# Prompt attention in the order in which it is written, on all engines and the sync queue

## The chip, the cores and the metric

The kernel runs on one core of one Trainium2 chip. The metric is the device time of one execution in microseconds (us). A core has five engines with an instruction stream each: PE (TensorE, matmuls and transposes), DVE (VectorE), ACT (ScalarE), POOL (GpSimd) and SP (SyncE, which here issues almost all DMAs). Each engine takes its own instructions in the order in which the built program holds them, and one that waits for another engine or for a DMA holds up all that stand behind it.

## The reference, cut to what matters

One layer of a hybrid trunk for a prompt of 2048 tokens and a small sample group. The part in question is the prompt's attention: 8 heads, and for each head three dilated patterns of 129 keys a query.

```
for (window, r) in ((128, 1), (512, 4), (2048, 16)):      # three patterns of each head
    scores = q . k[t], k[t-r], ..., k[t-window]  - slope * distance
    p = exp(scores - max);  out, lse = p @ v / sum(p), log-sum-exp
attn = sum over patterns of softmax(lse) * out
h = x + W_out [attn ; pool(n)]          # then y = h + ConvFFN(RMSNorm(h))
```

## The kernel before, in words

The kernel projects the prompt (queries, keys and values go to DRAM as `qT`, `kT`, `v_s`), does the attention, merges the three patterns and multiplies by `W_out`, and ends with the feed-forward part. This text is about the attention, from 447 to 813 us of the profiled execution.

Its work is a list of 192 **items**. Item `i` is two blocks of 128 queries of one head and one pattern, and each head has 24 items; head `h` begins at item 24 `h`. A block has one or two blocks of keys (narrow: 128 columns, wide: 256). An item goes through three steps, each an own function:

- `scores` (L289, L290): four matmuls into a PSUM tile `Sp` (four buffers); on DVE the bias and the minimum (`T`, `st`, L292); on ACT the exponential (`Pt`, L294).
- `turn` (L302): PE transposes `Pt` into a PSUM tile; the copy `PTs` out of it is on DVE for three items of four (L305) and on ACT for the fourth (L307).
- `values` (L324): matmuls with the value tile `V` into `Op`; ACT copies `Op` to `O` (L328), POOL adds `st` (L330), and after the last of a half, `store_o` sends `O` to DRAM on SP.

`advance(i)` writes down the scores of item `i`, the turn of item `i-2` and the values of item `i-3`, in this order. The first 8 calls of `advance` stand ahead of the changed loop. The loop calls `advance(i)` from 8 on, and writes other work ahead of some of the calls:

- at item 4 of head `h`, `load_head(h+1)`: six DMAs of 512 KB that bring the next head's `QK` tile (two buffers), and a bias table on POOL;
- at items of `NEXT_V`, `next_v`: the value tiles for the next pair of heads, 26 DMAs for each pair;
- `param_load` and `param_turn`, which bring parameters of the feed-forward part and transpose them on PE (L217);
- at items 150, 155, ..., 185 a piece of `W_out` for the next stage:

```
raw = p2.tile([P, CH], F32, tag="row", name="rawo", bufs=2)
nc.sync.dma_start(raw, wov[:, k, 0:CH])
split(wo0[k][:, 0, 0:CH], wo0[k][:, 1, 0:CH], raw)
```

`split` is a copy on ACT (L112, which waits for the DMA) and a subtraction on DVE (L113, which waits for the copy). In the kernel before, the written order is only a wish: the compiler's scheduler goes through the instructions with its own idea of how long each takes, and fixes the order on each engine. It places an instruction later than written where it takes its inputs to come late, and pulls others forward.

Of the kernel before, what the change touches and what calls it, by code (L numbers as in the profile page):

```python
# [9 lines left out]
F32 = mybir.dt.float32  # L10
# [7 lines left out]
P = 128  # L18
S = 2048
DM = 1024  # L20
KT = DM // P
H = 8
# [9 lines left out]
CH = 512  # L32
# [10 lines left out]
def f32(ap):  # L43
    return ap.bitcast(F32)
# [3 lines left out]
def kernel(ctx, tc, ins, cst, outs):  # L48
    nc = tc.nc
# [61 lines left out]
    def split(hi, lo, src, eng=None):  # L111
        nc.scalar.copy(hi, src)  # L112
        (eng or nc.vector).tensor_tensor(out=lo, in0=src, in1=f32(hi), op=ALU.subtract)  # L113
# [41 lines left out]
    def qk_tile():  # L155
        return pq.tile([P, 3, S], F32R, tag="QK", name="QK", bufs=2)

    def load_qk(h, qk, cols):
        rows = slice(h * DH, (h + 1) * DH)
        Q, KH, KL = (qk[:, i, cols] for i in range(3))  # L160
        nc.sync.dma_start(f32(Q[0:DH]), qT_hi[rows, cols])
        nc.sync.dma_start(f32(Q[DH:P]), qT_lo[rows, cols])
        for half in range(2):
            hr = slice(half * DH, (half + 1) * DH)
            nc.sync.dma_start(f32(KH[hr]), kT_hi[rows, cols])
            nc.sync.dma_start(f32(KL[hr]), kT_lo[rows, cols])

    def bias_table(h):
        tab = pq.tile([P, 3, 2 * P], F32, tag="tab", name="tab", bufs=2)
        nc.gpsimd.tensor_scalar(out=tab, in0=base, scalar1=2.0 ** -(h + 1), scalar2=None, op0=ALU.mult)  # L170
        return tab

    def value_tile(pool, tag):

        t = pool.tile([P, 8 if tag == "V" else 16, P + 2], F32, tag=tag, name="V", bufs=6 if tag == "V" else 1)
        nc.gpsimd.memset(t[:, :, 0:1], 1.0)
        nc.gpsimd.memset(t[:, :, P + 1:P + 2], 1.0)
        return t

    def load_v(hp, p, t, lo, hi):  # L180

        vs = v_s[:, hp * P:(hp + 1) * P]
        d = t[:, :, 1:P + 1]
        if p == 0:
            nc.sync.dma_start(d, vs.rearrange("(n i) f -> i n f", i=P)[:, lo:hi])
        else:
            r = DILS[p]
            n = min(r, hi - lo)
            for j in range(lo, hi, n):
                J, c = divmod(j, r)  # L190
                src = vs[J * P * r:(J + 1) * P * r].rearrange("(m c i) f -> i m c f", c=r, i=RUN)[:, :, c:c + n]
                for i in range(RUN):
                    nc.sync.dma_start(d[i::RUN, j - lo:j - lo + n, :], src[i])
# [4 lines left out]
    def param_load(j):  # L198
        n = 2 * NF if j < 4 else 2 * SB
        row = rows_of[j] = p2.tile([2 * NF, 4 * P], F32, tag="row", name="row", bufs=2)  # L200
        if j < 4:
            src = conv_b if j == 3 else conv_w[0, j:j + 1]
            nc.sync.dma_start(row[:, 0:P], src.rearrange("l (c p) -> (l c) p", p=P))
        else:
            nc.sync.dma_start(row[:n], stv[:, (j - 4) * 4 * P:(j - 3) * 4 * P])

    def param_turn(j):
        row = rows_of.pop(j)
        tp = psum.tile([P, 4, P], F32, tag="tp", name="tpc", bufs=4)
        if j < 4:  # L210
            n = 2 * NF
            nc.tensor.transpose(tp[:, 0, :n], row[:, 0:P], ident[:n, :n])
            nc.vector.tensor_copy(cw[:, j, :], tp[:, 0, :n])
        else:
            n = 2 * SB
            for c in range(4):
                nc.tensor.transpose(tp[:, c, :n], row[:n, c * P:(c + 1) * P], ident[:n, :n])  # L217
            nc.vector.tensor_copy(stT[:, 4 * j - 16:4 * j - 12, 0:n], tp[:, :, :n])
# [24 lines left out]
    def load_head(h):  # L243
        qk, tab = qk_tile(), bias_table(h)
        load_qk(h, qk, slice(0, S))
        heads[h] = (*(qk[:, i, :] for i in range(3)), tab)
# [3 lines left out]
    def next_v(hp, p, half):  # L250
        t = value_tile(p2, "V")
        load_v(hp, p, t, 8 * half, 8 * half + 8)
        for b in range(8):
            pair_v[hp, p, 8 * half + b] = t[:, b, :]
# [20 lines left out]
    def scores(it):  # L275
        h, p, pr = it
        tab = heads[h][3]
        if pr % 4 == 0:
            state["st", p] = pq.tile([P, 8], F32, tag="st", name="st", bufs=8)
        st = state["st", p]  # L280
        Sp = psum.tile([P, 2, 2 * P], F32, tag="mm", name="Sp", bufs=4)
        Pt = pq.tile([P, 2, 2 * P], F32, tag="P", name="Pt", bufs=3)
        blocks = []
        for s in range(2):
            idx = 2 * pr + s
            i8 = idx % 8
            q, kh, kl, kb = views(h, p, idx)
            w = P * len(kb)
            nc.tensor.matmul(Sp[:, s, :w], q, kh, start=True, stop=False)  # L289
            nc.tensor.matmul(Sp[:, s, :w], q, kl, start=False, stop=True)  # L290
            T = pq.tile([P, 2 * P], F32, tag="T", name="T", bufs=3)
            nc.vector.tensor_tensor_reduce(out=T[:, :w], in0=Sp[:, s, :w], in1=tab[:, p, 2 * P - w:], op0=ALU.add,  # L292
                                           op1=ALU.min, scale=1.0, scalar=3e38, accum_out=st[:, i8:i8 + 1])
            nc.scalar.activation(Pt[:, s, :w], T[:, :w], AF.Exp, bias=st[:, i8:i8 + 1], scale=-1.0)  # L294
            blocks += [(s, idx % 4, n, b, len(kb)) for n, b in enumerate(kb)]
        return st, Pt, blocks
# [40 lines left out]
    def turns(seq):  # L337
        at = {}
        for p in seq:
            n = at[p] = at.get(p, -1) + 1  # L340
            yield from ((p, 2 * n), (p, 2 * n + 1))

    ORDER = [(0, 0, 0, 0) + (2, 1) * 4] + [(0, 2, 1) * 4] * (H - 2) + [(0, 2, 2, 1, 2, 0, 2, 1, 0, 1, 1, 0)]
    items = [(h, p, pr) for h in range(H) for p, pr in turns(ORDER[h])]
    NI = 24
    AHEAD = 8
# [3 lines left out]
    def spread_next(i):  # L350
        if i < len(items):
            h, p, pr = items[i]
            if p and pr % 2 == 0:
                spread_q(h, p, pr // 2)

    def advance(i):
        if i >= AHEAD:
            spread_next(i + SPREAD)
        if i < len(items):
            attn[i] = scores(items[i])  # L360
        if 0 <= i - 2 < len(items):
            PTs[i - 2] = turn(items[i - 2], attn[i - 2])
        if 0 <= i - 3 < len(items):
            values(items[i - 3], attn.pop(i - 3), PTs.pop(i - 3))
# [4 lines left out]
    with tc.tile_pool(name="p1", bufs=1) as p1:  # L369
        raw, W_hi, W_lo = {}, {}, {}  # L370
# [326 lines left out]
    def act_tile(i):  # L697
        return (p4 if i % 2 else ph).tile([P, 2, 4, CH], F32R, tag="act", name="act", bufs=1)

    def load_pool(c):  # L700
        mB = act_tile(c)
        nc.sync.dma_start(f32(mB.rearrange("p a g t -> p (a g) t")),
                          pl_s.rearrange("(a p) t -> p a t", p=P)[:, :, c * CH:(c + 1) * CH])
        return mB

    mBs = {}
    wov = w_out0.rearrange("(k p) f -> p k f", p=P)


    with tc.tile_pool(name="p2", bufs=1, reuse_waits="tile") as p2:  # L710
        wo0 = [h_tile(k) for k in range(KT)]
        for half in range(2):
            for p in (2, 1):
                next_v(0, p, half)
        nc.vector.memset(stT[:, :, 2 * SB:], 0.0)
        for i in range(AHEAD, AHEAD + SPREAD):
            spread_next(i)
        NEXT_V = {(1, 14): (2, 0), (1, 17): (0, 0), (1, 21): (1, 0), (1, 23): (0, 1), (0, 1): (2, 1), (0, 3): (1, 1)}
        for i in range(AHEAD, len(items) + 3):
            if i < len(items):  # L720
                h, li = divmod(i, NI)
                if (i == AHEAD or h and li == 4) and h + 1 < H:
                    load_head(h + 1)

                if (h % 2, li) in NEXT_V and 0 < h < H - (h % 2):
                    next_v((h + 1) // 2, *NEXT_V[h % 2, li])
                j, r = divmod(i - NI, 8)
                if r == 0 and 0 <= j < 15:
                    param_load(j)
                if r == 5 and 0 < j < 16:  # L730
                    param_turn(j - 1)
                if i >= 150 and i % 5 == 0 and i < 190:
                    k = ((i - 150) // 5 + 4) % KT
                    raw = p2.tile([P, CH], F32, tag="row", name="rawo", bufs=2)
                    nc.sync.dma_start(raw, wov[:, k, 0:CH])
                    split(wo0[k][:, 0, 0:CH], wo0[k][:, 1, 0:CH], raw)
                if (h, li) == (7, 0):
                    mBs[0] = load_pool(0)
            advance(i)

    right.close()

# [548 lines left out]
```

## Time and profile before

| | |
|---|---|
| time, median of 3 runs | 2547.57 us (2534.75 to 2547.64) |
| profiled execution, its time | 2555.85 us |
| its span, first to last instruction | 2554.1 us |
| mean granted clock of TensorE | 0.98 |
| PE busy | 2510.9 us, 98% of the span |
| DVE, ACT, POOL busy | 1731.0, 1087.4, 186.4 us |

Busy is time in which an engine worked on an instruction of its own; for PE the ends of matmuls are modelled. The granted clock is the share of full speed that TensorE's clock had in a stretch: 1.00 is 2.4 GHz, 0.50 is 1.2 GHz. A busy PE at half the clock is busy with fewer instructions, so the two are read together.

### The profile page before, as it was taken

How to read it: one execution, taken by the hardware profiler on the slowest of the kernel's cores; microseconds unless marked ns; L12 is line 12 of the kernel's file. 1: busy time of each engine (PE TensorE's matmuls, PEld its weight loads, DVE VectorE, ACT ScalarE, POOL GpSimd, SP SyncE). 2: the span in 40 equal slices, each digit the busy share in tenths (PEclk: the TensorE clock that was granted, in tenths of full speed). 3: DMA queues.
4: the chain of work that ended last, by engine and by line, in shares of the span. 5: the costliest groups of instructions: out<-in, count | busy, mean ns of one | idle time of the engine just before them, and what ended most of it. 6: DMA issues, size and time to landing. Idle time of an engine off the chain costs nothing.

```text
span 2554.1 us, 36224 instructions
## 1 busy us (share of the span) xinstructions
PE 2510.9 (98%) x13310; PEld 2137.5 (84%) x13310; DVE 1731.0 (68%) x3819; ACT 1087.4 (43%) x2021; POOL 186.4 (7%) x246
## 2 busy tenths in 40 slices
PE   7999999999998999999999999999999999999999
PEld 5888887899997788788888888888888889999997
DVE  6445445465566785888987788887887666666655
ACT  6233332565565222543433454443443444445442
POOL 1111111222222100000000000000000000000000
PEclk9999999897799999999999999999999999999999
DMA  6333434865574998855558334447443446222321
GB/s 221 101 121 104 132 98 122 196 153 134 123 190 146 315 305 253 258 178 184 178 163 264 114 109 153 129 132 250 143 140 103 132 114 224 84 84 85 93 76 62
DMA packets 412876, 393.59 MB, mean 154 GB/s; under 512 B 16347, under 2 KB 319543, under 8 KB 410012
## 3 DMA queue, kind: packets, MB, share of 16 engines
q1 hardware_dynamic: 412476, 390.48, 50.3%
q8 instruction: 105, 1.72, 0.3%
q0 software_dynamic: 224, 0.80, 0.1%
q14 instruction: 71, 0.58, 0.1%
HBM read 305.70 MB, written 85.52 MB: 153 GB/s over the span
## 4 chain that ended last, share of the span: by engine, by line
PE 93%; DVE 2%; DMA 2%; issue 1%; ACT 1%; POOL 0%; SPq 0%; DVEq 0%; POOLq 0%; ACTq 0%
PE pu L1035 38%; PE pd L1211 19%; PE ps L470 13%; PE Op L324 5%; PE po L814 5%; PE tp L302 3%; PE Sp L289 3%; PE Sp L290 2%; PE tp L122 1%; PE tp L479 1%; PE pd L1205 1%; DMA om<-o_s 1%; DVE T L292 0%; PE pp L551 0%; DMA QK<-kT_lo 0%
## 5 line engine op out<-in xcount | busy, mean ns | idle before, releaser
L1035 PE MATMUL pu<-h,w 128*128 128x512 f32 (+1 forms) x5232 | 989.0, 349 | 1.7 <-ACT w L112 1.2
L1035 PEld LDWEIGHTS pu<-h,w 128*128 128x128 f32 x5232 | 849.9, 188 | 132.6 <-ACT w L112 1.6
L1211 PE MATMUL pd<-w,act 128*128 128x512 f32 x2112 | 490.2, 392 | 0.0
L1211 PEld LDWEIGHTS pd<-w,act 128*128 128x128 f32 x2112 | 396.6, 188 | 88.1
L112 ACT CAST w<-raw 128x1024 fp32r<-128x1024 f32 (+1 forms) x282 | 286.9, 1026 | 290.8 <-PE pd L1211 185.9
L113 DVE TENSOR_TENSOR w<-raw,w 128x1024 fp32r<-128x1024 f32 (+1 forms) x278 | 328.5, 1185 | 26.5 <-ACT w L112 26.3
L470 PE MATMUL ps<-W_hi,xh 128*128 128x512 f32 x1024 | 333.7, 399 | 1.0 <-ACT xh L112 1.0
L1179 DVE SCALAR_TENSOR_TENSOR cv<-ex,cw,cv 128x512 f32<-128x512 f32 x352 | 261.9, 744 | 27.7 <-ACT cv L1171 25.1
L1169 ACT COPY ex<-pu 128x512 f32<-128x512 f32 (+1 forms) x220 | 110.1, 500 | 333.9 <-PE pu L1035 333.6
L470 PEld LDWEIGHTS ps<-W_hi,xh 128*128 128x128 f32 x1024 | 193.3, 189 | 43.5 <-ACT xh L112 1.5
L292 DVE CUSTOM_DVE_ANT_0 T<-Sp,tab 128x256 f32<-128x256 f32 (+1 forms) x384 | 130.7, 364 | 131.8 <-PE Sp L290 93.7
L294 ACT ACTIVATE Pt<-T,st 128x256 f32<-128x256 f32 (+1 forms) x384 | 163.7, 459 | 94.1 <-DVE st L292 83.9
L470 PE MATMUL ps<-W_lo,xh 128*128 128x512 f32 x512 | 203.0, 396 | 0.0
L1213 DVE TENSOR_TENSOR ya<-ya,pd 128x512 f32<-128x512 f32 x192 | 130.6, 682 | 103.4 <-PE pd L1211 102.8
L95 POOL TENSOR_TENSOR rs<-ms,mhalf 128x8 f32<-128x8 f32 (+3 forms) x68 | 76.4, 1124 | 1584.5 <-DVE stT L1172 1046.8
L324 PE MATMUL Op<-V,PTs 128*128 128x65 f32 x1200 | 181.5, 287 | 1.6 <-DVE PTs L305 1.2
L324 PEld LDWEIGHTS Op<-V,PTs 128*128 128x128 f32 x1200 | 173.1, 213 | 3.0 <-DVE PTs L305 1.9
L1171 ACT ACTIVATE cv<-pu,cw 128x512 f32<-128x512 f32 (+3 forms) x264 | 166.0, 649 | 0.0
L112 ACT CAST act<-cv 128x512 fp32r<-128x512 f32 x88 | 54.6, 620 | 171.2 <-DVE cv L1188 165.0
L302 PE MATMUL tp<-ident,Pt 128*128 128x128 f32 x600 | 121.2, 302 | 3.1 <-ACT Pt L294 3.1
L470 PEld LDWEIGHTS ps<-W_lo,xh 128*128 128x128 f32 x512 | 97.0, 190 | 20.0
L1172 DVE COPY stT<-ex 128x2 f32<-128x2 f32 x176 | 28.5, 162 | 116.9 <-ACT ex L1169 116.9
(225 smaller groups left out, 2769.1 us busy)
## 6 DMA issues: line engine op xcount, KB each, us to landing
raw<-in_w_up_dram SPq DMA_DIRECT2D x176, 512.0 KB
raw<-in_w_down_dram SPq DMA_DIRECT2D x80, 512.0 KB
hn_s<-w SPq DMA_DIRECT2D x16, 1024.0 KB
h<-hn_s SPq DMA_DIRECT2D x32, 512.0 KB
far<-in_cache_k_dram SPq DMA_DIRECT2D x64, 256.0 KB
far<-in_cache_v_dram SPq DMA_DIRECT2D x64, 256.0 KB
om<-o_s SPq DMA_DIRECT2D x16, 792.0 KB
raw<-in_w_in_dram SPq DMA_DIRECT2D x16, 512.0 KB
```

The source lines that it names most:

```text
L112: nc.scalar.copy(hi, src)
L113: (eng or nc.vector).tensor_tensor(out=lo, in0=src, in1=f32(hi), op=ALU.subtract)
L292: nc.vector.tensor_tensor_reduce(out=T[:, :w], in0=Sp[:, s, :w], in1=tab[:, p, 2 * P - w:], op0=ALU.add, op1=ALU.min, scale=1.0, scalar=3e ...
L294: nc.scalar.activation(Pt[:, s, :w], T[:, :w], AF.Exp, bias=st[:, i8:i8 + 1], scale=-1.0)
L302: nc.tensor.transpose(tp[:, j, :], Pt[:, s, n * P:(n + 1) * P], ident)
L324: nc.tensor.matmul(Op[:, i4, :], PT[:, j, :], pair_v[hp, p, b][:, v0:v0 + DH + 1], start=n == 0, stop=n == m - 1)
L470: nc.tensor.matmul(ps, xh[:, a, k, :], (W_hi, W_lo)[b][j, k // 2][:, k % 2, :], start=n == 0, stop=n == 3 * KT - 1)
L1035: nc.tensor.matmul(ps[:, :n], w[:, a, k, :], hs[k][:, b, c0:c0 + n], start=i == 0, stop=i == 3 * KT - 1)
L1171: nc.scalar.activation(d, s, AF.Identity, bias=cw[:, 3, ct:ct + 1], scale=cw[:, 2, ct:ct + 1])
L1179: nc.vector.scalar_tensor_tensor(out=d, in0=e[j], scalar=cw[:, j, ct:ct + 1], in1=d, op0=ALU.mult, op1=ALU.add)
L1211: nc.tensor.matmul(ps, act[0][:, a, k, tau * P:(tau + 1) * P], wd[k][:, b, :], start=k == 0 and j == 0, stop=k == n - 1 and j == 2)
L1213: nc.vector.tensor_tensor(out=ysl, in0=ysl, in1=ps, op=ALU.add)
```

## The change

The loop is put into `with tc.manual_schedule():`. Nothing else is edited; the rest of the diff is the loop's indentation. In the block, the scheduler no longer chooses: on every engine and on SP, instructions stand in the order in which the Python code writes them. What stands ahead of the block and behind it is scheduled as before.

```
-        for i in range(AHEAD, len(items) + 3):
-            if i < len(items):
...
-            advance(i)
+
+        with tc.manual_schedule():
+            for i in range(AHEAD, len(items) + 3):
+                if i < len(items):
+                    h, li = divmod(i, NI)
+                    if (i == AHEAD or h and li == 4) and h + 1 < H:
+                        load_head(h + 1)
...
+                    if i >= 150 and i % 5 == 0 and i < 190:
+                        k = ((i - 150) // 5 + 4) % KT
+                        raw = p2.tile([P, CH], F32, tag="row", name="rawo", bufs=2)
+                        nc.sync.dma_start(raw, wov[:, k, 0:CH])
+                        split(wo0[k][:, 0, 0:CH], wo0[k][:, 1, 0:CH], raw)
...
+                advance(i)
```

Three places of the built programs show what moves. The first is PE where head 2 ends and head 3 begins (`QK_5340` is head 3's tile in the first listing and `QK_5342` in the second; a number behind a name is a buffer's or a tile's). Before:

```order
L289 MATMUL Sp_5814<-QK_4704,qs_5640 128x256
L290 MATMUL Sp_5814<-QK_4704,qs_5640 128x256
L289 MATMUL Sp_5837<-QK_5340 128x128
L289 MATMUL Sp_5860<-QK_5340 128x256
L289 MATMUL Sp_5887<-QK_5340,qs_5733 128x128
L290 MATMUL Sp_5837<-QK_5340 128x128
L290 MATMUL Sp_5860<-QK_5340 128x256
L290 MATMUL Sp_5887<-QK_5340,qs_5733 128x128
L217 MATMUL tpc_5759<-ident_63,row_5439 128x16 x4
L302 MATMUL tp2_5777<-ident_63,Pt_5709 128x128 x4
L324 MATMUL Op_5784<-V_5194,PTs_5752 128x65 x4
L302 MATMUL tp2_5803<-ident_63,Pt_5736 128x128 x2
```

Score matmuls of six items (`Sp_5765`, `Sp_5791` and `Sp_5814`, which begin ahead of these rows, and the three shown of head 3) follow each other with no transpose between them, and only then come transposes again. The same items in the change, at the last item of head 2 and the first of head 3:

```order
L302 MATMUL tp2_5828<-ident_63,Pt_5768 128x128 x2
L324 MATMUL Op_5833<-V_5247,PTs_5808 128x65 x2
L289 MATMUL Sp_5839<-QK_5342 128x128
L290 MATMUL Sp_5839<-QK_5342 128x128
L289 MATMUL Sp_5839<-QK_5342 128x256
L290 MATMUL Sp_5839<-QK_5342 128x256
L302 MATMUL tp2_5851<-ident_63,Pt_5794 128x128 x4
L324 MATMUL Op_5833<-V_5247,PTs_5831 128x65 x2
L289 MATMUL Sp_5862<-QK_5342 128x256
L290 MATMUL Sp_5862<-QK_5342 128x256
```

Four score matmuls, one item's transposes and one item's value matmuls now alternate through the whole loop.

The second place is ACT at the first copy of a piece of `W_out`. Before, where the item of `Pt_8334` is the first of head 7:

```order
L328 COPY O_8223<-Op_8375 128x4x65
L294 ACTIVATE Pt_8334<-T_8337,st_8332 128x128
L112 CAST h_4177<-rawo_7889 128x512
L112 CAST h_4178<-rawo_8007 128x512
L294 ACTIVATE Pt_8334<-T_8342,st_8332 128x256
L294 ACTIVATE Pt_8357<-T_8360,st_8332 128x256
```

In the change, where `Pt_7896` belongs to item 150:

```order
L294 ACTIVATE Pt_7871<-T_7874,st_7841 128x128
L294 ACTIVATE Pt_7871<-T_7879,st_7841 128x128
L112 CAST h_4177<-rawo_7891 128x512
L294 ACTIVATE Pt_7896<-T_7899,st_7710 128x256
L294 ACTIVATE Pt_7896<-T_7904,st_7710 128x256
L307 COPY PTs_7910<-tp2_7907 128x256
L328 COPY O_7887<-Op_7888 128x4x65
```

The first copy moves from item 168 to item 150, ahead of that item's exponentials; the seven that follow stand five items apart. The subtractions on DVE move with them, each ahead of its item's `T`.

The third place is SP at the last `load_head`, as a piece of the difference (line numbers behind the block grow by 2):

```order
 L165 DMA QK<-kT_hi 64x2048
 L166 DMA QK<-kT_lo 64x2048
-L735 DMA rawo<-in_w_out_dram 128x512 x2
+L737 DMA rawo<-in_w_out_dram 128x512 x4
 L702 DMA act<-pl_s 128x8x512
-L735 DMA rawo<-in_w_out_dram 128x512 x4
+L737 DMA rawo<-in_w_out_dram 128x512 x2
 L233 DMA o_s<-O 128x8x132
-L735 DMA rawo<-in_w_out_dram 128x512 x2
+L737 DMA rawo<-in_w_out_dram 128x512
 L227 DMA o_s<-O 128x8x132
```

SP's order hardly changes: the first piece of `W_out` stands behind the six `QK` transfers in both, and the two last pieces now stand behind one more store each.

## Rows read from the trace of the kernel before

**Rows 1.** The page: busy time of PE, and the granted clock in 40 slices.
```profile
PE 2510.9 (98%) x13310; PEld 2137.5 (84%) x13310; DVE 1731.0 (68%) x3819; ACT 1087.4 (43%) x2021; POOL 186.4 (7%) x246
PEclk9999999897799999999999999999999999999999
```

**Rows 2.** Windows: busy us (x instructions) of each engine, clock, DMA share, GB/s.
```profile
core 0: us, PE busy (x) PEld busy (x) DVE busy (x) ACT busy (x) POOL busy (x), PEclk, DMA share, GB/s
560.00:570.00 10.00, 10.00 (x90) 9.88 (x89) 6.57 (x31) 7.05 (x17) 0.00 (x0) 1.00 0.73 150
580.00:590.00 10.00, 10.00 (x51) 10.00 (x49) 3.34 (x13) 3.92 (x11) 1.66 (x1) 0.50 1.00 210
```

**Rows 3.** Timeline of PE at the starts of heads 3 and 5: start, length, idle before.
```profile
573.10 0.38 PE L289 MATMUL Sp<-QK,qs 128*128 128x256 f32 x1 [0.85 <-DVE st L292]
574.59 0.58 PE L289 MATMUL Sp<-QK,qs 128*128 128x256 f32 x1 [0.98 <-DVE st L292]
...
665.87 0.39 PE L289 MATMUL Sp<-QK,qs 128*128 128x256 f32 x1 [0.84 <-DVE st L292]
667.36 0.39 PE L289 MATMUL Sp<-QK,qs 128*128 128x256 f32 x1 [0.98 <-DVE st L292]
```

**Rows 4.** Half-microsecond windows at which the granted clock falls and comes back.
```profile
498.50:499.00 0.50, 0.50 (x4) 0.29 (x2) 0.43 (x3) 0.29 (x1) 0.00 (x0) 0.50 1.08 246
512.00:512.50 0.50, 0.50 (x6) 0.50 (x6) 0.50 (x5) 0.00 (x0) 0.12 (x1) 0.87 0.00 0
573.50:574.00 0.50, 0.11 (x1) 0.00 (x0) 0.25 (x1) 0.00 (x0) 0.50 (x2) 0.57 0.00 0
604.00:604.50 0.50, 0.50 (x6) 0.50 (x4) 0.24 (x1) 0.00 (x0) 0.00 (x0) 0.71 0.00 0
668.00:668.50 0.50, 0.50 (x6) 0.41 (x5) 0.00 (x0) 0.00 (x0) 0.50 (x1) 1.00 0.00 0
696.00:696.50 0.50, 0.50 (x5) 0.50 (x4) 0.50 (x5) 0.29 (x1) 0.20 (x1) 0.54 0.00 0
781.50:782.00 0.50, 0.00 (x0) 0.00 (x0) 0.00 (x0) 0.50 (x2) 0.00 (x0) 0.79 0.94 250
788.50:789.00 0.50, 0.50 (x6) 0.50 (x5) 0.42 (x1) 0.50 (x3) 0.00 (x0) 0.89 0.00 0
```

**Rows 5.** Windows of L289 alone: the count is of score matmuls, two an item.
```profile
440.00:733.00 293.00, 101.40 (x301) 62.12 (x301) 0.86 0.66 157
440.00:761.00 321.00, 112.93 (x336) 68.69 (x336) 0.87 0.68 163
```

**Rows 6.** Timeline of SP's DMA issues around the last load of a head.
```profile
736.48 0.60 SPq L161 DMA_DIRECT2D QK<-qT_hi  x1
...
739.69 0.59 SPq L166 DMA_DIRECT2D QK<-kT_lo  x1
740.33 1.06 SPq L735 DMA_DIRECT2D rawo<-in_w_out_dram  x2
```

**Rows 7.** The chain that ended last: the wait for one piece of `W_out`.
```profile
776.61 4.81 DMA rawo<-in_w_out_dram
```

**Rows 8.** Windows where the data rate of the DMA engines steps up.
```profile
752.00:754.00 2.00, 2.00 (x20) 2.00 (x20) 1.29 (x7) 2.00 (x6) 0.00 (x0) 1.00 0.86 195
754.00:756.00 2.00, 2.00 (x21) 2.00 (x20) 1.73 (x7) 1.16 (x3) 1.01 (x2) 1.00 1.06 366
```

**Rows 9.** Groups on ACT and DVE from 745 to 812 us: busy, mean ns, idle before.
```profile
L294 ACT ACTIVATE Pt<-T,st 128x256 f32<-128x256 f32 x40 | 18.8, 504 | 6.8 <-DVE st L292 6.7
L112 ACT CAST h<-rawo 128x512 fp32r<-128x512 f32 x8 | 4.8, 617 | 1.7 <-DMA rawo<-in_w_out_dram 1.7
L307 ACT COPY PTs<-tp 128x256 f32<-128x256 f32 x4 | 1.5, 367 | 1.5 <-PE tp L302 1.4
...
L292 DVE CUSTOM_DVE_ANT_0 T<-Sp,tab 128x256 f32<-128x256 f32 x39 | 15.5, 422 | 13.6 <-PE Sp L290 9.4 <-PE tp L302 3.4 <-ACT Pt L294 0.4
L113 DVE TENSOR_TENSOR h<-rawo,h 128x512 fp32r<-128x512 f32 x8 | 5.5, 693 | 2.1 <-ACT h L112 2.1
```

**Rows 10.** Timeline of PE in head 7, the longest wait there.
```profile
782.41 0.47 PE L302 MATMUL tp<-ident,Pt 128*128 128x128 f32 x1 [2.23 <-ACT Pt L294]
```

More of the change, by code (lines that the diff above doesn't have):

```diff
@@ L718 @@
         NEXT_V = {(1, 14): (2, 0), (1, 17): (0, 0), (1, 21): (1, 0), (1, 23): (0, 1), (0, 1): (2, 1), (0, 3): (1, 1)}
-        for i in range(AHEAD, len(items) + 3):
-            if i < len(items):
[L721 to L738, printed above, removed]
-            advance(i)
+        with tc.manual_schedule():
[4 more added lines that the diff above has]
+                        load_head(h + 1)
+                    if (h % 2, li) in NEXT_V and 0 < h < H - (h % 2):
+                        next_v((h + 1) // 2, *NEXT_V[h % 2, li])
+                    j, r = divmod(i - NI, 8)
+                    if r == 0 and 0 <= j < 15:
+                        param_load(j)
+                    if r == 5 and 0 < j < 16:
+                        param_turn(j - 1)
+                    if i >= 150 and i % 5 == 0 and i < 190:
[3 more added lines that the diff above has]
+                        split(wo0[k][:, 0, 0:CH], wo0[k][:, 1, 0:CH], raw)
+                    if (h, li) == (7, 0):
+                        mBs[0] = load_pool(0)
+                advance(i)
     right.close()
```

## The prediction

> **What bounds the kernel now.** The page comes first: PE is busy for 98% of the span, so only PE's time counts, and other engines matter where PE waits for them [rows 1]. The slices of the granted clock, though, are below 9 in three places, the slices from 447 to 511 and from 575 to 702 us, all within the attention. So the next view is windows of 10 us over the attention, and there the reader sees two kinds of stretch, both with PE busy for all of the 10 us: from 560 to 570 us it does 90 matmuls at full clock, from 580 to 590 it does 51 at half clock [rows 2]. A microsecond at half clock thus does 51/90 of the work and loses 1 - 51/90 = 0.43 us. Then the timeline of PE shows what came ahead: at the starts of heads 3 and 5 two waits each, 0.85 and 0.98 us, then 0.84 and 0.98 us, for DVE to be done with an `Sp` tile [rows 3]. Right behind the second wait the clock falls, at about 573.6 us, and comes back at 604.1; the second time it is at full until 668.5 and back at 696.5; two other drops last from 498.5 to 512.1 and from 781.7 to 788.6 us [rows 4]. Outside such stretches PE has no gap worth a name and the attention is bound by PE at full clock.
>
> The pace comes from counting score matmuls, two an item: 301 have begun by 733 us and 336 by 761 [rows 5], so 17.5 items take 28 us, 1.6 us an item. Item 150 (the 301st) begins between 732 and 733; I use 732.5. Head 7 (the 337th) begins at 761.
>
> **The change part by part.** No instruction is added or removed; the order differs inside the loop alone.
>
> *The bursts at heads 3 and 5 go.* `Sp` has four buffers, and a burst of scores with no transposes runs into DVE, which frees them. In the written order four score matmuls alternate with one item's transposes and values, so PE has two items of other work, 3.2 us at the pace, between an item's scores and its transposes. The way through DVE and ACT takes for a wide item 0.42 + 0.50 + 0.50 us (its second `T` runs beside the first exponential) [rows 9], 1.4 us, so it is hidden; if that cover went, its 1.4 us would show in each item. Gain: waits 0.85 + 0.98 + 0.84 + 0.98 = 3.65 us; half clock 30.5 + 28.0 = 58.5 us times 0.43 = 25.2 us. Sum -28.8 us. What is late next there is the `QK` tile of the odd head; it is asked for 20 items (32 us) ahead, and I cost it at zero for that.
>
> *The first piece of `W_out` is waited for.* The written order puts ACT's copy ahead of item 150's exponentials, and DVE's subtraction ahead of its `T`. SP issues that DMA behind the last `QK` load: the six issues run from 736.48 us on, the `W_out` issue is at 740.33 [rows 6], 8 us after PE begins item 150. Before, this cost nothing, since the copy stood at item 168. What queues behind it: on ACT all exponentials from item 150 on, on DVE all `T`; PE can still do the scores of 150 and 151, the turns of 148 and 149 and the values of 147, and stops at the values of 148, about 1.9 us into item 150, at 734.4 us. After the landing come copy 0.62, subtraction 0.69, one `T` 0.42, two exponentials 0.50 each, and the copy `PTs` of item 148, 0.37 on ACT [rows 9], 3.1 us together. When does it land? The lower bound is a piece that had the queue to itself, 4.81 us from issue to copy [rows 7]: 740.33 + 4.81 = 745.1, PE idle 745.1 + 3.1 - 734.4 = 13.8 us. The upper bound is that it comes after the 3 MB of `QK`: the data rate is 195 GB/s until 754 us and 366 from there [rows 8], the step between `QK` (64 partitions a DMA) and the load of `act` issued next. Landing at 754 gives 754 + 3.1 - 734.4 = 22.7 us. I take 22.7, because one DMA queue served both and the step is a clean one.
>
> That is where a rule of the Trainium skill bears, and it speaks against the change: "DMA: Bandwidth & Descriptors", section "Queues, rings and completion order", says that each DMA engine takes descriptors in ring order and that all DMAs issued from SP share one row of rings. By that rule the landing is 754 us; by the lone piece alone it would be 745.1, and the whole sum 8.9 us smaller. The step in the data rate agrees with the rule.
>
> *The clock after it.* PE idle this long will be followed by half clock, as the waits of 1.8 us were. The four periods seen last 13.6, 30.5, 28.0 and 6.9 us [rows 4], mean 19.8: +8.5 us, bounds 3.0 and 13.1.
>
> *Head 7.* Two more pieces stand on SP behind a store: that of item 180 behind a store written in `advance(176)`, that of item 185 behind one of `advance(184)`. A store follows the values and the copy `O` of its `advance`, so it leaves about 2 us into it; the piece lands 4.8 us later, 6.8 us into that `advance`. For item 185 that is 6.8 + 3.1 - 1.6 - 1.9 = 6.4 us of PE idle; for 180, four items later, 6.8 + 3.1 - 6.4 - 1.9 = 1.6 us. With one average period of half clock: 8.0 + 8.5 = 16.5 us. Before, the same stretch had a wait of 2.23 us for a piece [rows 10] and 6.9 us of half clock, 2.23 + 3.0 = 5.2 us. Net +11.3 us; bounds 0 (SP early by the 4.8 us) and +20 (a long period).
>
> *The other five pieces* (155 to 175) have landed by then or are issued ten items ahead: zero, hidden by 16 us; if not, the 3.1 us chain each.
>
> *Heads 0 and 1.* The drop at 498.5 us follows gaps under half a microsecond at the start of head 1. In the written order PE may instead stand at head 1's first scores until its `QK` has landed. I put zero; bounds -13.6 x 0.43 = -5.8 (the drop goes) and +8.5 (one average period more).
>
> *SP and POOL.* SP's order is the same but for the pieces and stores named; POOL's copies stand six items ahead of their use in both, 9.6 us of cover, so zero.
>
> Sum: -28.8 + 22.7 + 8.5 + 11.3 + 0 = +13.7 us on the profiled execution's 2555.85 us. That execution lies 8.3 us above the median of the runs; the difference is carried to the median: 2547.6 + 13.7 = **2561 us**.
>
> **The rivals.** *SP is early* (not slower). The place is SP at `load_head(7)` and at head 7's stores: if the written order hands SP its tiles and copies sooner, SP is not the 8 us late that rows 5 and 6 show. On time it issues the first `QK` transfer at item 148, 732.5 - 3.2 = 729.3 us and not 736.5, so the piece lands 7.2 us sooner, item 150 costs 15.5 us, and head 7's pieces, sooner by more than 4.8 us, net zero: -28.8 + 15.5 + 8.5 = -4.8, 2543 us. It decides from about 5 us on: 5 us off item 150 and all of head 7's 11.3 outweigh the +13.7. Against it: SP issues back to back there, six transfers in 3.85 us and the piece next [rows 6], which its own pace sets and not a release. *The bursts were not the cause*: PE would then stand at heads 3 and 5 in any order, say for the head's `QK`, and the 28.8 us are not gained: 2561 + 29 = 2590 us. Against it: rows 3 name DVE, not a DMA. *The written order starves PE in the middle heads*: waits of a few tenths each item keep the clock at half. A head takes 24 x 1.6 = 38.4 us; at half clock 38.4 x 90/51 = 67.8, so +29 us a head, and two heads so give 2561 + 59 = 2620 us. For it: the drop at 498.5 us came after small gaps; against it: 1.4 us of way under 3.2 us of cover. *Nothing moves*: the order of PE changes in every item, so this is only the case in which the terms cancel, 2548 us, inside the forecast's own spread.
>
> **How the numbers follow.** Forecast 0.50, SP early 0.25, bursts not the cause 0.12, starved heads 0.13. A measurement of this kernel can tell about 0.5%, 12.7 us, from no change: 2534.8 and 2560.3 are the limits. The forecast's own range goes from 2544 (item 150's clock and head 7 at their low bounds: -5.5 - 11.3) to 2575 (clock +4.6, head 7 +8.7), so 0.26 of its 0.50 lies above 2560.3 and 0.24 within. SP early spreads from 2532 (a short period of half clock, -5.5, and head 1's drop gone, -5.8) to 2550: 0.10 faster, 0.15 within. The two others, 0.25, are slower. Together: faster 0.10, same 0.39, slower 0.51. The range of 8 in 10 reaches from 2533 (the low end of SP early) to 2597 (bursts not the cause, and the spread behind it); the starved heads lie above it.
>
> **What would show it.** In the changed kernel's profile: no wait over 0.3 us of PE on DVE at the starts of heads 3 and 5, and no half clock behind them; a wait of ACT's copy L112 for the `rawo` DMA of some 20 us in head 6, with PE idle for nearly as long; two shorter ones in head 7, for a sum of about 8 us on PE; half clock after the first. The prediction is wrong if the copy at item 150 waits under 10 us, if the clock stays at full after it, or if PE has small gaps in every item of heads 2 to 5.

## The result and the profile after

The changed kernel takes 2926.34 us (median of 4 runs, 2923.6 to 2930.08); beside it the kernel before took 2541.16 us (4 runs). The ratio is 1.152, 95% interval 1.147 to 1.158: slower by 385 us, where 2561 us was forecast and 2597 was the upper end of the range.

The page first, the rows that answer to [rows 1]; the lower one is the granted clock in 40 slices of the span (2928.3 us):

```profile
PE 2762.1 (94%) x13310; PEld 2355.7 (80%) x13310; DVE 1750.5 (60%) x3819; ACT 1108.0 (38%) x2021; POOL 184.3 (6%) x246
PEclk9999996555555555999999999999999999999999
```

PE does the same 13310 matmuls and is "busy" for 251 us more. The clock is at 6 in one slice and at 5 in the nine behind it, 439 to 1171 us: nearly the whole attention runs at 0.50. The windows that answer to [rows 2] (us, busy us with the count of instructions, granted clock, DMA share, GB/s):

```profile
560.00:570.00 10.00, 8.34 (x35) 0.50 0.18 56
580.00:590.00 10.00, 8.47 (x37) 0.50 0.48 124
```

The count tells more than the busy share: 35 and 37 matmuls in 10 us, against 90 at full clock and 51 at half clock [rows 2]. So half clock is not all of it; PE also has some 1.6 us of gaps in each 10. The list of waits from 447 to 1200 us (engine, line, releaser: us in sum, times, longest) names them:

```profile
DVE T L292 <- PE Sp L290: 414.2, 362, 4.5
PEld Sp L289 <- DVE st L292: 177.0, 188, 15.4
PE Sp L289 <- DVE st L292: 131.1, 186, 15.1
```

PE waits for DVE 186 times, about once in each of the loop's 184 items, and DVE waits for PE 362 times. They take turns. In its own attention, from 447 to 813 us, the kernel before has 17 such waits of PE:

```profile
PE Sp L289 <- DVE st L292: 7.5, 17, 1.0
```

The timeline of PE over an item of the changed kernel (start, length, in brackets the idle time ahead and what ended it), and of DVE in the same stretch:

```profile
700.42 0.56 PE L289 MATMUL Sp<-QK,qs 128*128 128x256 f32 x1
700.78 0.41 PE L290 MATMUL Sp<-QK,qs 128*128 128x256 f32 x1
701.83 0.58 PE L289 MATMUL Sp<-QK,qs 128*128 128x256 f32 x1 [0.63 <-DVE st L292]
702.20 0.41 PE L290 MATMUL Sp<-QK,qs 128*128 128x256 f32 x1
702.42 0.63 PE L302 MATMUL tp<-ident,Pt 128*128 128x128 f32 x2
702.84 0.95 PE L324 MATMUL Op<-V,PTs 128*128 128x65 f32 x4
703.55 0.45 PE L289 MATMUL Sp<-QK 128*128 128x128 f32 x1
...
704.75 0.58 PE L289 MATMUL Sp<-QK 128*128 128x256 f32 x1 [0.53 <-DVE st L292]
```

```profile
701.34 0.42 DVE L292 CUSTOM_DVE_ANT_0 T<-Sp,tab 128x256 f32<-128x256 f32 x1 [2.13 <-PE Sp L290]
701.69 0.08 DVE L292 DVE_READ_ACCUMULATOR2_ANT st<- 128x1 f32 x1
702.76 0.42 DVE L292 CUSTOM_DVE_ANT_0 T<-Sp,tab 128x256 f32<-128x256 f32 x1 [0.99 <-PE Sp L290]
```

The wait stands between the two blocks of one item. The first block's matmuls end at 701.2, DVE reads the first half of `Sp` from 701.34 to 701.76, and only then do the second block's matmuls begin, at 701.83. Yet they write the other half. The transposes and values of older items, which wait for nothing, stand behind the second block in PE's order and can't fill the gap.

One piece of what was forecast is there too. ACT's copy of the first `W_out` piece waits for the DMA, and PE behind it:

```profile
1014.47 0.62 ACT L112 CAST h<-rawo 128x512 fp32r<-128x512 f32 x1 [14.21 <-DMA rawo<-in_w_out_dram]
```

```profile
1016.21 0.58 PE L289 MATMUL Sp<-QK 128*128 128x256 f32 x1 [15.11 <-DVE st L292]
```

### The profile page after: what moved, and what is told of

The parts are those of the page before. It is cut to its first block, busy times and chain, and to the rows that moved or that the text cites. A ratio compares the mean times of both kernels' runs of the same rounds, so it can differ in the third digit from the quotient of the medians.

```text
span 2928.3 us, 36228 instructions
## 1 busy us (share of the span) xinstructions
PE 2762.1 (94%) x13310; PEld 2355.7 (80%) x13310; DVE 1750.5 (60%) x3819; ACT 1108.0 (38%) x2021; POOL 184.3 (6%) x246
## 4 chain that ended last, share of the span: by engine, by line
PE 88%; DVE 4%; issue 3%; DMA 3%; POOL 1%; SPq 0%; ACT 0%; DVEq 0%; POOLq 0%; ACTq 0%
PE pu L1037 34%; PE pd L1213 17%; PE ps L470 11%; PE Op L324 7%; PE po L816 5%; PE Sp L289 5%; PE tp L302 4%; PE Sp L290 3%; DVE T L292 2%; PE tp L122 1%; PE tp L479 1%; PE pd L1207 1%; DMA rawo<-in_w_out_dram 1%; DMA QK<-kT_lo 1%; PE pp L551 0%
## 5 line engine op out<-in xcount | busy, mean ns | idle before, releaser
L292 DVE CUSTOM_DVE_ANT_0 T<-Sp,tab 128x256 f32<-128x256 f32 (+1 forms) x384 | 140.1, 366 | 421.6 <-PE Sp L290 414.2
L294 ACT ACTIVATE Pt<-T,st 128x256 f32<-128x256 f32 (+1 forms) x384 | 176.6, 462 | 411.4 <-DVE st L292 411.4
L324 PEld LDWEIGHTS Op<-V,PTs 128*128 128x128 f32 x1200 | 273.0, 326 | 0.1
L324 PE MATMUL Op<-V,PTs 128*128 128x65 f32 x1200 | 269.2, 394 | 0.0
L289 PE MATMUL Sp<-QK,qs 128*128 128x128 f32 (+1 forms) x256 | 128.9, 504 | 74.4 <-DVE st L292 74.4
L302 PE MATMUL tp<-ident,Pt 128*128 128x128 f32 x600 | 166.0, 415 | 0.0
L289 PEld LDWEIGHTS Sp<-QK,qs 128*128 128x128 f32 x256 | 78.7, 308 | 104.1 <-DVE st L292 103.7
L289 PE MATMUL Sp<-QK 128*128 128x256 f32 (+1 forms) x128 | 69.6, 550 | 61.3 <-DVE st L292 56.7
```

Of the source, the lines that this page charges most:

```text
L302: nc.tensor.transpose(tp[:, j, :], Pt[:, s, n * P:(n + 1) * P], ident)
L324: nc.tensor.matmul(Op[:, i4, :], PT[:, j, :], pair_v[hp, p, b][:, v0:v0 + DH + 1], start=n == 0, stop=n == m - 1)
```

## The experiments

Theory A: the second block's matmuls wait until DVE has read the first block, because both write one `Sp` tile; in the written order nothing stands between. Theory B: the transposes come too early, two items behind their scores. Theory C: the half clock comes from the stalls at the loop's start and at the `W_out` piece, and the small waits follow. Medians; "before" in these groups was 2545 to 2547 us.

**Two tiles.** Each block gets a tile of its own, still four buffers:

```
-        Sp = psum.tile([P, 2, 2 * P], F32, tag="mm", name="Sp", bufs=4)
         for s in range(2):
...
-            nc.tensor.matmul(Sp[:, s, :w], q, kh, start=True, stop=False)
...
+            Sp = psum.tile([P, 4 * P], F32, tag="mm", name="Sp", bufs=4)
+            nc.tensor.matmul(Sp[:, :w], q, kh, start=True, stop=False)
...
```

> The changed kernel, with a score tile Sp of its own (512 columns, four buffers as before) for each of an item's two blocks. Theory A (shared tile): in the changed kernel the second block's matmuls wait till DVE has read the first block, since both lie in one Sp tile; this wait of some 0.6 us stands in each item and keeps the clock at 0.50. It is gone here: under 15 waits of PE on DVE at L289 and its successor lines over 0.3 us outside heads' starts, attention from 447 to some 830 us instead of 1180, time 2500 to 2590 us. Theory B (lag too short: the transposes come two items behind their scores, too early): nothing here alters that, time 2900 to 2950 us. Theory C (the half clock comes from the stall for the W_out piece and from the starts of heads, and the small waits follow from it): 2900 to 2950 us.

Measured: 2552.66 us, ratio to before 1.003 (1.001 to 1.005). Theory A holds, B and C fall: neither the lag nor the stalls were touched, and 374 us went. PE has no wait for DVE at L289 from 445 to 830 us; it still stands for 24.2 us at the first `W_out` piece. A window in the middle of the attention (columns as in [rows 2]):

```profile
600.00:610.00 10.00, 10.00 (x92) 9.88 (x90) 7.39 (x32) 6.39 (x17) 2.94 (x11) 1.00 0.48 130
```

**Scores first.** The tile stays shared; the order within an item changes:

```
         for s in range(2):
...
             nc.tensor.matmul(Sp[:, s, :w], q, kl, start=False, stop=True)
...
+        for s in range(2):
+            i8, w = (2 * pr + s) % 8, ws[s]
             T = pq.tile([P, 2 * P], F32, tag="T", name="T", bufs=3)
...
             nc.scalar.activation(Pt[:, s, :w], T[:, :w], AF.Exp, bias=st[:, i8:i8 + 1], scale=-1.0)
```

> The changed kernel, with one shared Sp tile as it was, but all four score matmuls of an item written ahead of its two DVE instructions. Theory A (shared tile, wait of the second block's matmuls on DVE's reading of the first): no DVE instruction stands between the two blocks any more, so the wait is gone as with two tiles; 2500 to 2590 us, and within 15 us of the kernel with two tiles. If two tiles help and this does not, it is the count of tiles in flight and not the order within an item. Theory B (lag too short): 2900 to 2950 us, or longer, since DVE starts later in the item.

Measured: 2557.01 us, ratio 1.005 (1.003 to 1.006), 4 us from the kernel with two tiles. So the wait needs both: a tile that the two blocks share, and a reader written between its two writers. Either edit takes it away.

**A longer lag.** `turn(items[i - 3])` and `values(items[i - 4])` in place of 2 and 3; `Pt` with 4 buffers, `PTs` with 3.

> The changed kernel with its scores untouched, but the transposes three items behind the scores instead of two, and the values four (one more Pt buffer, one PTs buffer less). Theory A (shared tile): the wait within an item stays, time 2890 to 2960 us, clock 0.50 through the attention. Theory B (lag too short): the small waits go, time under 2650 us.

Measured: 2926.4 us (one run), the time of the changed kernel, and the same list of waits of PE from 447 to 1200 us:

```profile
PE Sp L289 <- DVE st L292: 129.9, 186, 17.8
```

Theory B is wrong.

**Scores first in the scheduler's order.** The same edit in the kernel before, without the block of written order.

> The kernel before (the scheduler's order), with all four score matmuls of an item written ahead of its two DVE instructions. Theory A (shared tile): the scheduler already put other items' work between the two blocks, so the edit removes no wait there: 2515 to 2570 us, within 1% of the kernel before. Rival: the wait on the first block also cost the scheduler's order something (its bursts at heads 3 and 5): 2500 to 2520 us, with the half clock at 575 and 668 us gone.

Measured: 2507.43 us, ratio 0.985 (0.982 to 0.987). The rival was right and my expectation wrong: the shared tile cost the kernel before too. Two windows (columns as in [rows 2]) over the stretch that held two half-clock periods [rows 4]:

```profile
600.00:650.00 50.00, 49.22 (x439) 48.51 (x439) 33.16 (x152) 32.65 (x86) 16.89 (x28) 1.00 0.76 175
650.00:700.00 50.00, 50.00 (x448) 49.56 (x448) 33.87 (x159) 33.81 (x91) 16.70 (x33) 1.00 0.68 171
```

The clock is at 1.00 from 570 to 700 us. Of the 17 waits of `Sp` for DVE in the kernel before, 7.5 us in sum, this one has none.

**Work between the blocks.** The changed kernel, but `mid()`, between the first and the second block, now calls `turn(i - 2)` and `values(i - 3)`.

```
             blocks += [(s, idx % 4, n, b, len(kb)) for n, b in enumerate(kb)]
+            if s == 0:
+                mid()
```

> The changed kernel with one shared Sp tile and DVE's two instructions each behind its own block, as they were; but the transposes and values of the earlier items are written between the two blocks' matmuls instead of behind both. Theory A (the second block's matmuls wait for DVE's reading of the first, and in the written order nothing lies between them): the wait has an item's other PE work, about 0.8 us, to hide under, so 2540 to 2580 us, as with two tiles. Rival (a shared tile costs its wait wherever the other work stands, since 0.8 us of cover is too short for the way from matmul to DVE and back): 2800 us and more.

Measured: 2574.31 us, ratio 1.011 (1.006 to 1.015). As theory A says: from 600 to 650 us PE is busy for 49.45 us at a clock of 1.00, with nothing removed from the program. The last 22 us against two tiles are explained in part: seven of PE's waits for DVE at L289, 12.9 us in sum, come between 738 and 809 us, each at the second block of an item with a `W_out` piece (155, 160, ..., 185); with two tiles PE waits there for 6.6 us, in head 7.

**Late copy.** Two tiles, and `split` of each `W_out` piece written nine items behind its DMA.

```
                 if i >= 150 and i % 5 == 0 and i < 190:
...
-                    split(wo0[k][:, 0, 0:CH], wo0[k][:, 1, 0:CH], raw)
+                if i >= 159 and i % 5 == 4:
+                    split(wo0[k][:, 0, 0:CH], wo0[k][:, 1, 0:CH], raws.pop(k))
```

> The kernel with two score tiles, and in it the split of each W_out piece written nine items behind its DMA instead of right behind it. Theory (terms of the prediction: ACT's copy in the written order waits for the first piece, and PE behind it): the kernel with two tiles shows PE waits of 24.2 us at item 150 and 8.5 us in head 7, and stretches at half clock behind them, 17 us at 0.50 (7 us lost) and some 20 us between 770 and 800 us (8 us lost); they go, so 2553 - 24 - 8 - 15 = 2506 us, range 2495 to 2522. Rival (PE waits there for something else, such as the QK of head 7, which shares the queue): the wait at item 150 moves but stays, 2535 to 2560 us.

Measured: 2529.83 us, ratio 0.995 (0.992 to 0.997); 23 us of the 47 that I expected. ACT's copy still waits, 9.73 us in place of 22.9:

```profile
717.31 0.62 ACT L112 CAST h<-rawo 128x512 fp32r<-128x512 f32 x1 [9.73 <-DMA rawo<-in_w_out_dram]
```

SP issued that piece at 702.70 us, so it took 14.6 us to land, and nine items (14.4 us) counted from item 150, which PE began before SP was there, were too few. PE's wait behind it fell from 24.2 to 10.1 us, so it follows the place of the copy, as the theory says; the delay was mis-sized.

**Written order on PE alone.** `tc.manual_schedule(engines={PE})`, with two tiles and with the shared tile; and the reverse, all engines but PE, with the shared tile.

> The kernel with two score tiles, with PE alone in the written order and ACT, DVE, POOL and SP in the scheduler's. Theory (the loss left with two tiles is ACT's and DVE's place of the W_out copy, not PE's order): the copies stand where the scheduler puts them, no PE wait over 10 us in head 6, 2500 to 2525 us. Rival (PE's written order costs it in itself): 2545 to 2565 us, as with all engines in written order.

> The changed kernel's shared tile, with PE alone in the written order and the other engines in the scheduler's. Theory A (PE's order puts the second block's matmuls straight behind the first's, and a PE that is held there is held whatever the others do): wait in each item and half clock through the attention, 2870 to 2930 us, less than the changed kernel by the 14 us W_out wait at most and what follows it. Rival (all engines' order is needed): under 2700 us, as with all engines but PE, 2681.

> The changed kernel (shared tile) with ACT, DVE, POOL and SP in the written order and PE in the scheduler's. Theory A (the harm is in PE's order, where nothing lies between the two blocks): no small wait in each item and no lasting half clock; what is left is the W_out copy's wait, 2540 to 2600 us. Rival (DVE's written order, one item after the other, does the harm whatever PE's order): over 2800 us.

Measured: PE alone with two tiles 2507.69 us, ratio 0.984 (0.981 to 0.988); PE alone with the shared tile 2899.56 us, ratio 1.140 (1.134 to 1.145); all but PE 2681.29 us, ratio 1.052 (1.048 to 1.056). PE's written order with the shared tile is enough for most of the loss, 354 of 385 us, and without the shared tile it loses nothing. With two tiles PE's longest wait from 690 to 780 us is 0.8 us there: the wait for the `W_out` piece belongs to ACT's and DVE's order. All but PE fits neither expectation. PE waits for DVE at L289 68 times there (61.8 us, 20.8 of them at the `W_out` piece); why the scheduler's order of PE meets waits against DVE's written one stays open.

**Waits in a part of the items.** Scores first, except that DVE reads between the blocks in each 4th item, in each 2nd, from head 3 on, or up to head 2:

```
+            if s or counts["n"] % 4 == 0:      # or % 2 == 0, > 72, <= 72
+                read()
```

> The kernel with the scores written first, except that each fourth item has DVE's reading between its two blocks again, as in the changed kernel: 46 of the 184 items in the loop keep the wait. Theory (most of the loss is the half clock that the waits bring, and sparse waits do not bring it): 46 waits at 0.6 us or somewhat more are 28 to 45 us, so 2585 to 2602 us with the clock at 1.00 between them. Rival (each wait costs the 2.0 us an item that the changed kernel loses, (2926 - 2557) / 184): 2557 + 92 = 2649 us. Second rival (a wait now and then is enough to keep the clock down): over 2750 us.

> As the kernel with the wait in each fourth item, but in each second: 92 waits. If the waits are charged at 0.6 to 1 us at full clock: 2557 + 55 to 92 = 2612 to 2649 us. If each costs the 2.0 us of the changed kernel: 2741 us. If the clock falls and stays down: some 2860 us, since each item then lasts 2.7 us at half clock and the waits are added.

Measured: 2603.74 us (ratio 1.023, 1.018 to 1.028) and 2635.17 us (1.036, 1.030 to 1.041). Above the 2557 us with no such wait that is 46.7 us for 46 waits and 78 us for 92: 1.0 and 0.85 us each, not the 2.0 us of the changed kernel. Timeline of PE and a window, each 2nd item:

```profile
604.86 0.33 PE L299 MATMUL Sp<-QK,qs 128*128 128x128 f32 x1 [0.50 <-DVE st L289]
608.00 0.39 PE L299 MATMUL Sp<-QK 128*128 128x256 f32 x1 [0.64 <-DVE st L289]
```

```profile
570.00:620.00 50.00, 42.35 (x350) 1.00 0.47 103
```

The waits are as long as in the changed kernel, but the clock is at 1.00 there, and from 484 to 753 us. From the first score matmul of item 48 to that of item 120 all three are at full clock: scores first takes 117.2 us (532.33 to 649.50), with 18 waits 127.1 (553.64 to 680.70), with 36 waits 141.6 (546.92 to 688.53), so 0.55 and 0.68 us a wait. What is above that in the 1.0 and 0.85 goes with half clock elsewhere: with each 4th it lasts from 463 to 514 us at the loop's start (463 to 480 with scores first), and with each 2nd for 68 us in head 7, behind a wait of 1.74 us at 806.43 (791 to 797 with scores first):

```profile
808.00:876.00 68.00, 55.64 (x252) 0.50 0.13 37
```

So waits in a part of the items did not take the clock down in the middle heads, but half clock that had begun lasted longer beside them.

> Scores written first in heads 0 to 2, and DVE's reading between the two blocks, as in the changed kernel, in every item from head 3 on (120 items). The clock is at full when these waits begin. Theory 1 (a wait in every item takes the clock down by itself): it falls to 0.50 at the start of head 3 and stays there till the attention's end; 120 x 2.0 us = 240, 2557 + 240 = 2797 us, 2760 to 2830. Theory 2 (a wait in every item keeps the clock down but does not take it down; that took the long waits for QK at the loop's start): it stays at 1.00 until PE's wait for the W_out piece at item 150, so 78 x 0.85 + 42 x 2.0 = 150 us, 2707 us, 2680 to 2730.

Measured: 2792.02 us, ratio 1.097 (1.084 to 1.110), theory 1's 2797. Timeline of PE at the start of head 3, then windows:

```profile
574.94 0.39 PE L299 MATMUL Sp<-QK 128*128 128x256 f32 x1 [0.53 <-DVE st L289]
577.20 0.39 PE L299 MATMUL Sp<-QK 128*128 128x256 f32 x1 [0.64 <-DVE st L289]
...
584.37 0.33 PE L299 MATMUL Sp<-QK,qs 128*128 128x128 f32 x1 [0.53 <-DVE st L289]
```

```profile
575.00:580.00 5.00, 3.86 (x30) 1.00 0.96 221
580.00:585.00 5.00, 3.97 (x33) 0.96 1.01 210
585.00:590.00 5.00, 4.50 (x23) 0.50 0.88 180
```

No wait over 0.64 us stands there; five items with the wait, and the clock falls at about 584.6 us. Here waits of this length in each item took it down by themselves.

> The reverse: DVE's reading between the blocks in every item of heads 0 to 2 (64 items of the loop), scores written first from head 3 on. Theory 1 and theory 2 alike (the clock falls at the loop's start and cannot come back while the waits go on, and comes back when they end): clock 0.50 from some 465 us on through heads 1 and 2, back at 1.00 within 40 us of head 3's first item; 64 x 2.0 = 128 us, 2557 + 128 = 2685 us, 2660 to 2710. Rival (once down in the attention the clock stays down whatever the waits): over 2850 us.

Measured: 2695.29 us, ratio 1.059 (1.047 to 1.071). PE's last such wait ends at 698.23; the windows behind it:

```profile
695.00:700.00 5.00, 4.37 (x22) 0.50 0.01 3
700.00:705.00 5.00, 5.00 (x25) 0.50 0.93 197
...
720.00:725.00 5.00, 5.00 (x45) 0.98 0.02 3
```

The clock comes back some 20 us after the waits end. It doesn't stay down by itself.

**Two tiles in the scheduler's order.**

> The kernel before (the scheduler's order) with a score tile for each block, four of them as with two tiles in the written order. Theory (in the scheduler's order too it was the wait on the first block that made its bursts at heads 3 and 5 run into DVE, as the kernel with scores first in that order showed with 2507 us): 2500 to 2520 us, no half clock between 570 and 700 us. Rival (with scores first it gained by four items of tiles in flight; four tiles of one block each hold but two items, so the bursts run into DVE sooner): 2540 us or more.

Measured: 2506.11 us, ratio 0.985 (0.981 to 0.989), as the theory says; from 570 to 700 us the clock is at 1.00. Only two items' tiles are in flight there, so it is the sharing and not the number of buffers that made the bursts wait. This version, that with scores first, and PE alone in written order with two tiles are faster than the kernel before by some 1.5%, and can't be told apart.

## Why the prediction was wrong

**The step that failed** is the one that costs the written order's cover: "PE has two items of other work, 3.2 us at the pace, between an item's scores and its transposes. ... so it is hidden". It followed one dependency, scores to DVE to ACT to transposes, and that one is hidden: a longer lag changed nothing. It took the four score matmuls of an item for one block with nothing inside. There is a second dependency within the item: the code writes DVE's reading of the first half of `Sp` ahead of the matmuls that write the second half, and program order keeps that, at a cover of nothing. The 1.4 us of "if that cover went, its 1.4 us would show in each item" priced another way, through DVE and ACT; the wait that came is on DVE alone, 0.50 to 0.64 us long, and costs 2.03 us an item with the clock that goes with it.

A rule bears on it. The Trainium skill, "PSUM — Partial Sum Buffer", section "PSUM bank collisions raise a hardware error", says that accesses of two engines have to be kept apart by semaphores per PSUM bank and quadrant of partitions (per bank alone is its simpler form), not per address; by the table of its section "Specifications (TRN2)" the shared tile, 512 float32 columns, has the size of one bank. The runs agree that disjoint halves do wait (0.50 to 0.64 us) and that tiles of 512 columns each do not. Whether it is the tile or the bank that is guarded, they can't tell: two tiles in one bank were not tried. The Trainium skill's "Perfetto Trace Analysis", section "Matmuls", advises to rotate independent matmul groups through different banks. Two tiles did that for an item's blocks, for 374 us in the written order and 39 us in the scheduler's; but scores first, with the tile still shared, got 369 and 38 us, so by the runs the order within an item is about as good a cure.

**The price.** Per item the changed kernel loses (2926.34 - 2552.66)/184 = 2.03 us. At full clock the wait in every item costs 0.76: the four items from 574.94 to 584.37 last 2.36 us each, against 1.6 at the pace. The rest is the clock: an item of 1.6 us lasts 1.6 x 90/51 = 2.82 at half clock [rows 2], 1.22 more. Together 1.98, so by this estimate 184 waits cost 140 us by themselves and 225 us by the clock. In the middle of the attention it is more: from item 48 to item 144 an item of the changed kernel lasts 3.80 us (612.73 to 977.78), with two tiles 1.59 (529.80 to 682.11). Of the 2.22 between them 1.22 is the clock again, so at half clock the wait itself costs about 1.0. The mean over the loop is lower because the kernel with two tiles has half clock and the longer `W_out` wait of its own. The rival "starves PE in the middle heads" had the clock's part of this, 29 us a head, from gaps in each item that it left unexplained; it was given two heads and no price for the waits, and a chance of 0.13, because the cover argument spoke against it. The last of the prediction's own signs of being wrong, "small gaps in every item of heads 2 to 5", is what came.

**It was in the rows.** The waits at heads 3 and 5 [rows 3] were read as a burst that runs into four buffers. PE's order of the kernel before, at that place, shows what they are (number in the program, line, tile):

```
1951 L289 MATMUL Sp_5814<-QK_4704,qs_5640 128x256
1952 L290 MATMUL Sp_5814<-QK_4704,qs_5640 128x256
1953 L289 MATMUL Sp_5765<-QK_4704,qs_5585 128x128
1954 L290 MATMUL Sp_5765<-QK_4704,qs_5585 128x128
1955 L289 MATMUL Sp_5791<-QK_4704,qs_5640 128x256
1956 L290 MATMUL Sp_5791<-QK_4704,qs_5640 128x256
1957 L289 MATMUL Sp_5814<-QK_4704,qs_5640 128x256
```

The waits at 573.10 and 574.59 us are those of rows 1955 and 1957, the second blocks of `Sp_5791` and `Sp_5814`: they wait for DVE to read the first blocks (the trace has these shapes in this order from 571.42 to 574.59 us). A tile that had been given out already can't have waited for a buffer. The scheduler put other items' blocks in between, and where these ran out the wait showed. Written order takes those blocks away in every item. The clock, too, is read a little late in the prediction: at 573.6 us it falls as the second wait begins, which ends at 574.59, and not behind it.

**The other terms** can be checked in the kernel with two tiles, where the failed step doesn't hide them. PE's longest waits there:

```profile
717.86 1.11 PE L324 MATMUL Op<-V,PTs 128*128 128x65 f32 x4 [24.22 <-ACT PTs L307]
...
773.86 1.75 PE L324 MATMUL Op<-V,PTs 128*128 128x65 f32 x8 [1.91 <-DVE PTs L305]
791.27 1.97 PE L324 MATMUL Op<-V,PTs 128*128 128x65 f32 x8 [4.66 <-DVE PTs L305]
```

- *The first piece of `W_out`*: 22.7 us forecast, 24.2 measured. Its DMA was issued at 700.25 and ACT's copy began at 714.92, 14.7 us later (13.7 forecast from [rows 6] and [rows 8]; a lone piece took 4.81 [rows 7]). So it did land behind the `QK` transfers: the DMA engines move over 200 GB/s until 712 us. That agrees with what the prediction cites from the Trainium skill, "DMA: Bandwidth & Descriptors", section "Queues, rings and completion order". From the copy to PE's next matmul 2.9 us (3.1 forecast).
- *The clock after it*: at 0.50 until 733.2 us, 15.3 us of work, 6.6 us lost (8.5 forecast).
- *Head 7*: waits of 1.91 + 4.66 = 6.6 us (1.6 + 6.4 = 8.0 forecast) and about 17 us at half clock, 7.4 lost (8.5 forecast).
- *The bursts at heads 3 and 5*: in the windows of 10 us from 570 to 690 the clock is at 1.00; the -28.8 us were gained, for another reason than given.
- *Heads 0 and 1*: half clock from about 460 to 480 us. The forecast counted 13.6 us there in the kernel before [rows 4] and overlooked some 10 us more, from 447.3 to 457.5; over the windows of 10 us from 440 to 520 the clock's shortfall comes to 24 us at half clock in both kernels. So the term is zero, as it was put.

With these the sum is -28.8 + 24.2 + 6.6 + (6.6 + 7.4 - 5.2) + 0 = +10.8 us, where +13.7 was forecast; measured, two tiles are 2552.66 - 2545.2 = 7.5 us slower than before (1.5 to 12.2 by the interval). The agreement is partly luck. Between the two profiled executions, from which the terms are read, the difference is 2554.84 - 2555.85 = -1.0 us. From the first score matmul of item 8 to that of item 150 two tiles gained 35.9 us (465.70 to 732.25 before, 460.93 to 691.55 now), 7 more than the bursts' 28.8, and from there to the attention's last value matmuls (812.67, 808.49) they lost 36.5, where 22.7 + 8.5 + 11.3 = 42.5 was forecast; the rest of the difference lies outside the loop. What the 7 us are stays open; PE has 5.8 us less idle time there, of which the forecast counted 3.65. So the prediction describes, in its main terms, a kernel in which an item's blocks don't share a tile.

## What to carry to other kernels

Before instructions are taken in program order, list for each engine every pair of neighbours in the code between which another engine must act, within an iteration too, and count what lies between them: two halves of one PSUM tile with a read of the first written ahead of the second's matmul are such a pair. A wait that a scheduler's order shows only here and there may be one that it hides everywhere else; look which instruction waits, and on which earlier use of the same tile. Where PE's gaps are small but come in each iteration, read the granted clock beside them: here it made 0.76 us into 2. That held with the waits in every item; in a part of the items they cost 0.55 to 0.68 us each while the clock was at full.

## What was not expected

- Waits of 0.50 to 0.64 us in each second item left the clock at 1.00 from 484 to 753 us; in each item they took it to 0.50 behind the fifth, some 10 us after the first, and it came back some 20 us after they ended. With waits in each second item a half clock that began in head 7 lasted 68 us.
- A PE that the page shows as 94% busy had lost 385 us: the count of matmuls in a window (35 for 90) told it, the busy share (8.3 of 10 us) hardly.
- The tuned kernel before carried the same wait, 17 times in its attention, 7.5 us in sum, and by the medians lost 1.5% by it, some 38 us. In the profiled execution 25 us go with the half clock at heads 3 and 5; its time lies 8 to 11 us above the medians, and the kernel's runs spread from 2528 to 2559 us, with a mean clock of 0.992 in the run of 2529.33 and 0.978 in that of 2559.06.
